# A weight stream whose rounded half is written by a converting DMA of the GpSimd queue

## The chip, the cores and the metric

The kernel runs on one core of a Trainium2 chip, as one program in one launch. The core has a TensorE for matrix products (PE in the profile, with PEld for its weight loads), a VectorE (DVE), a ScalarE (ACT), a GpSimd (POOL), a SyncE (SP) that here only issues transfers, and 16 DMA engines that all queues share. Each of these engines executes its own instructions in order. The metric is the time of one execution on the device in microseconds. Lower is better.

## The reference, cut to what matters

The program is a trunk of two decoder layers over 512 tokens with a model width of 1024, all in float32.

```python
for l in range(DEPTH):                       # DEPTH = 2
    hn = rms_norm(h, attn_norm[l])
    proj = hn @ w_in[l]                      # 1024 x 2592
    y_a = rwkv7_mixer(proj[..., :896], ...)  # 4 heads, a recurrence over the tokens
    y_b = retention_mixer(proj[..., 896:1920], positions)
    y_c = mla_mixer(proj[..., 1920:], ...)   # 8 heads of latent attention
    mix = concatenate([y_a, y_b, y_c], axis=-1)
    h = h + mix @ w_out[l]                   # 1024 x 1024
    hn = rms_norm(h, ffn_norm[l])
    gu = hn @ w_gate_up[l]                   # 1024 x 5632
    h = h + (silu(gu[..., :2816]) * gu[..., 2816:]) @ w_down[l]   # 2816 x 1024
return rms_norm(h, final_norm)
```

## The kernel before, in words

Activations lie transposed, features on the 128 partitions and the 512 tokens along the free dimension. Every large product is made in three passes. An operand is split into a rounded half `hi`, of type float32r, and the rest `lo = x - hi`; the product is then `hi*hi + hi*lo + lo*hi`. In `gemm` (L385) these are three matmuls for each slice of 128 input features, the third of which reads `lo` of the weights. A block of 8 slices is therefore 24 matmuls of 128 x 128 by 512 columns.

The weights were put by the host into the order in which they are used, in one long array, and pass through the chip as a stream of blocks, most of them 128 x 1024 values (512 KB). `load_next` (L361) handles one block. It takes three tiles, each from three buffers: `wr` for the raw float32 values, `wh` for `hi`, `wl` for `lo`. SP loads `wr` from HBM (L373), ACT copies it with a conversion into `wh` (L376), and DVE subtracts to make `wl` (L377). Four blocks, listed in POOL_LO, subtract on POOL. The first two blocks are handled in two parts each.

`wnext` (L380) hands out one block and calls `load_next` so that the next ones are under way: at most three blocks are ready at a time. As `wh` and `wl` have three buffers, the writing of block n+2 waits until TensorE has finished block n-1, and has the time of blocks n and n+1 to be done.

Each layer has two stages. In the mixing stage (some 280 us a layer) the input projection, the three mixers and the output projection are interleaved: the generator `dense` (L899) issues the stream's products, and generators for the recurrence (`rwkv`, `chain` with L741, L746 and L750), retention and attention (`head`, L865 to L870) are woven between them by a driver with a table `T` of waiting times. In the FFN stage, gate and up blocks (L1188 to L1193) alternate, in groups of 8, 8 and 6 feature blocks, and after each group come 8 blocks of the down projection, each added into the residual stream on DVE (L1197). In the FFN POOL multiplies gate and up (L1191), ACT rounds the result (L286) and DVE makes its rest (L287).

The order of TensorE's instructions is that of the program text. On the other engines a planner places each instruction by its own costs once it sees the inputs of that instruction as ready, so their order can differ from that of the text. On the chip each engine then keeps the planner's order and waits where an input is late.

Of the kernel before, what the change touches and what calls it, by code (L numbers as in the profile page):

```python
# [178 lines left out]
def tile_trunk(ctx: ExitStack, tc: tile.TileContext, a: dict, out: bass.AP, dbg=None):  # L179
    nc = tc.nc  # L180
    act, dve, pool, sp = nc.scalar, nc.vector, nc.gpsimd, nc.sync
# [20 lines left out]
    def nm(s):  # L202
        uid[0] += 1
        return f"{s}_{uid[0]}"
# [156 lines left out]
    def load_next(parts=1):  # L361
        if stream["next"] < len(shapes):
            i, j = shapes[stream["next"]]
            stream["next"] += 1
            t = wp.tile([P, i * j], F32, tag="wr", name=nm("wr"), bufs=NW)
            src = a["wts"][stream["off"] : stream["off"] + P * i * j].rearrange("(p n) -> p n", p=P)
            stream["off"] += P * i * j
            hi = wp.tile([P, i * j], F32R, tag="wh", name=nm("wh"))
            lo = wp.tile([P, i * j], F32R, tag="wl", name=nm("wl"))
            on = stream["next"] - 1  # L370
            for part in range(parts):
                z = slice(part * i * j // parts, (part + 1) * i * j // parts)
                stream["dma"] = sp.dma_start(t[:, z], src[:, z])  # L373
                if parts > 1:
                    tc.keep_in_program_order(stream["dma"])
                act.copy(hi[:, z], t[:, z])  # L376
                (pool if on in POOL_LO else dve).tensor_tensor(lo[:, z], t[:, z], hi[:, z].bitcast(F32), ALU.subtract)  # L377
            stream["ready"].append(tuple(z.rearrange("p (i j) -> p i j", i=i) for z in (hi, lo)))

    def wnext():  # L380
        while len(stream["ready"]) < 3 and stream["next"] < len(shapes):
            load_next()
        return stream["ready"].pop(0)
# [515 lines left out]
    def dense():  # L899
# [3 lines left out]
        for k in range(KT):  # L903
            if k < 2:
                tc.keep_in_program_order(sp.dma_start(h[0][:, k, :], a["xT"][:, k, :]))
                load_next(2) if k == 0 else None
            elif k % 2 == 0:
                tc.keep_in_program_order(sp.dma_start(h[k // 2], a["xT"][:, k : k + 2, :]))
                load_next(2) if k == 4 else None
            xg.append(pair(ua))  # L910
            act.activation(xg[k][0], hk(k), AF.Identity, scale=col("attn_norm", 0, k))
            dve.scalar_tensor_tensor(xg[k][1], hk(k), col("attn_norm", 0, k), xg[k][0].bitcast(F32), ALU.mult, ALU.subtract)
# [342 lines left out]
```

## Time and profile before

| | |
|---|---|
| time, median of 3 runs | 1383.34 us (1379.25 to 1384.71) |
| the profiled execution | 1382.67 us, its span 1380.9 us |
| TensorE (PE) busy | 1313.5 us, 95% of the span |
| VectorE (DVE) busy | 796.2 us, 58% |
| ScalarE (ACT) busy | 569.7 us, 41% |
| GpSimd (POOL) busy | 238.7 us, 17% |
| the copies into `wh` (L376, ACT) | 206, 208.2 us busy |
| the subtractions into `wl` (L377, DVE) | 202, 283.3 us busy |
| moved by DMA | 130.84 MB, 95 GB/s over the span |

The profile is that of one execution. Busy time is the time in which an engine executes an instruction; DMA-issuing instructions and waits aren't counted. In a group line the name of a tile stands without its number, so `wh` is any of its buffers, and "a<-b" says that a is written from b. The number after the bar is the busy time of the group, then the mean of one instruction in ns, then the idle time of the engine just before these instructions and which instruction ended it. A timeline row has start (us from the span's start), duration, engine, line and shape, and in brackets the idle time before it. The chain is the sequence of instructions and transfers that ended last, followed back from the end, so its shares say which lines set the time.

### The profile page before, as it was taken

The numbers are of one execution on the slowest core, as the hardware profiler recorded it, in microseconds if no ns is written. First come the engines' busy times: TensorE is split into PE (matmuls) and PEld (weight loads), VectorE is DVE, ScalarE is ACT, GpSimd is POOL, SyncE is SP. The second block draws the span as 40 slices with busy tenths as digits, with TensorE's granted clock in tenths as the row PEclk, the third lists the DMA queues.
The fourth block names the chain that finished last, engine by engine and source line by source line (L and its number), as shares of the span: only waits on it lengthen the run. The fifth ranks groups of instructions, "written<-read, shape, count | busy, mean of one in ns | idle before, by whom it ended". The sixth has DMA issues, their size and how long they took to land.

```text
span 1380.9 us, 16829 instructions
## 1 busy us (share of the span) xinstructions
PE 1313.5 (95%) x6478; PEld 1055.3 (76%) x6478; DVE 796.2 (58%) x1183; ACT 569.7 (41%) x944; POOL 238.7 (17%) x181
## 2 busy tenths in 40 slices
PE   7989988899999999999999898889999999999996
PEld 5778766578888888888877776756888888888884
DVE  7787856747544445344757696476564534543543
ACT  7844445826322232122575335367342212321333
POOL 1160321213110011001314401112131101100111
PEclk9999999999999999999999899999999999999998
DMA  6434421212222232322532424021233223333221
GB/s 235 125 99 140 96 76 32 77 61 92 97 102 92 92 107 92 101 97 73 174 97 81 111 85 85 31 85 54 76 107 105 94 92 95 104 93 105 89 80 61
DMA packets 65577, 130.84 MB, mean 95 GB/s; under 512 B 29044, under 2 KB 31764, under 8 KB 65496
## 3 DMA queue, kind: packets, MB, share of 16 engines
q1 hardware_dynamic: 64120, 128.14, 30.2%
q8 instruction: 51, 0.84, 0.3%
q10 hardware_dynamic: 1232, 1.09, 0.2%
q0 software_dynamic: 144, 0.52, 0.1%
q14 instruction: 30, 0.25, 0.1%
HBM read 117.40 MB, written 9.18 MB: 92 GB/s over the span
## 4 chain that ended last, share of the span: by engine, by line
PE 80%; DVE 10%; ACT 5%; issue 3%; POOL 1%; DMA 1%; SPq 0%; DVEq 0%; ACTq 0%; POOLq 0%
PE pd L232 72%; PE pm L232 7%; PE pm L239 1%; DVE wl L377 1%; DVE nmx L865 1%; DVE Sb L750 1%; ACT u L867 1%; ACT wh L376 1%; DVE u L608 1%; DMA wr<-in_wts_dram 0%; DVE r L296 0%; ACT L327 0%; ACT u L882 0%; DMA u<-in_xT_dram 0%; DVE u L609 0%
## 5 line engine op out<-in xcount | busy, mean ns | idle before, releaser
L232 PE MATMUL pd<-u,wh 128*128 128x512 f32 x3048 | 959.9, 396 | 7.6 <-ACT wh L376 6.4
L232 PEld LDWEIGHTS pd<-u,wh 128*128 128x128 f32 x3048 | 570.0, 189 | 135.3 <-issue 8.0
L232 PE MATMUL pd<-u,wl 128*128 128x512 f32 x1524 | 597.7, 392 | 0.0
L376 ACT CAST wh<-wr 128x1024 fp32r<-128x1024 f32 (+3 forms) x206 | 208.2, 1013 | 531.9 <-PE pd L232 353.9
L232 PEld LDWEIGHTS pd<-u,wl 128*128 128x128 f32 x1524 | 288.5, 189 | 61.0 <-DVE wl L377 0.2
L377 DVE TENSOR_TENSOR wl<-wr,wh 128x1024 fp32r<-128x1024 f32 (+3 forms) x202 | 283.3, 1404 | 59.8 <-ACT wh L376 57.0
L1191 POOL TENSOR_TENSOR r<-r,r 128x512 f32<-128x512 f32 x44 | 63.7, 1447 | 576.2 <-ACT wh L376 484.6
L1190 DVE TENSOR_TENSOR r<-pd,rB 128x512 f32<-128x512 f32 x44 | 30.4, 691 | 135.4 <-PE pd L232 135.4
L1197 DVE TENSOR_TENSOR u<-u,pd 128x512 f32<-128x512 f32 x48 | 33.0, 687 | 125.9 <-PE pd L232 125.9
L232 PE MATMUL pm<-u,u 32*32 32x32 f32 (+4 forms) x728 | 77.2, 287 | 24.9 <-DVE Sb L750 16.2
L232 PEld LDWEIGHTS pm<-u,u 32*32 32x32 f32 (+3 forms) x728 | 55.1, 162 | 48.6 <-DVE Sb L750 21.5
L316 POOL TENSOR_TENSOR acc<-acc,r 128x512 f32<-128x512 f32 x37 | 55.2, 1491 | 192.5 <-ACT r L315 192.1
L1188 DVE TENSOR_TENSOR r<-pd,rB 128x512 f32<-128x512 f32 x44 | 30.4, 691 | 67.7 <-PE pd L232 67.5
L286 ACT CAST u<-r 128x512 fp32r<-128x512 f32 x52 | 32.4, 623 | 78.5 <-POOL r L1191 63.5
L232 PE MATMUL pd<-u,u 96*128 96x512 f32 (+3 forms) x128 | 45.2, 459 | 2.7 <-ACT u L867 1.6
L287 DVE TENSOR_TENSOR u<-r,u 128x512 fp32r<-128x512 f32 x52 | 35.9, 689 | 18.9 <-ACT u L286 18.9
L239 PE MATMUL pm<-ident,u 128*128 128x128 f32 x188 | 33.5, 283 | 5.5 <-ACT r L773 2.0
L870 POOL TENSOR_SCALAR u<-u,rs 128x384 f32<-128x384 f32 x16 | 20.6, 1285 | 98.8 <-DVE rs L869 67.6
L865 DVE TENSOR_REDUCE nmx<-pd 128x1 f32<-128x256 f32 (+3 forms) x64 | 30.0, 481 | 11.7 <-PE pd L232 11.2
L239 PEld LDWEIGHTS pm<-ident,u 128*128 128x128 f32 x188 | 23.7, 145 | 13.1 <-ACT r L773 3.3
L321 DVE SCALAR_TENSOR_TENSOR u<-u,PC,u 128x512 fp32r<-128x512 f32 x24 | 32.0, 1342 | 2.6 <-ACT u L320 2.5
L867 ACT ACTIVATE u<-pd,nmx 128x512 f32<-128x512 f32 (+2 forms) x48 | 26.0, 546 | 11.9 <-DVE nmx L865 7.8
(243 smaller groups left out, 1142.9 us busy)
## 6 DMA issues: line engine op xcount, KB each, us to landing
wr<-in_wts_dram SPq DMA_DIRECT2D x174, 512.0 KB, 3.5
wr<-in_wts_dram SPq DMA_DIRECT2D x22, 384.0 KB, 3.1
u<-in_xT_dram SPq DMA_DIRECT2D x7, 512.0 KB, 6.7
tb<-tab_d SPq DMA_DIRECT2D x8, 256.0 KB, 4.9
r<-r SPq DMA_DIRECT2D x32, 64.0 KB, 2.0
h_d<-u SPq DMA_DIRECT2D x4, 512.0 KB, 2.6
u<-h_d SPq DMA_DIRECT2D x4, 512.0 KB, 3.6
wr<-in_wts_dram SPq DMA_DIRECT2D x4, 432.0 KB, 3.1
```

Of the source, the lines that this page charges most:

```text
L232: tc.keep_in_program_order(nc.tensor.matmul(o, lhsT, rhs, start=start, stop=stop, skip_group_check=True))
L239: tc.keep_in_program_order(nc.tensor.transpose(o, x, idn))
L286: act.copy(hi, src)
L287: E("e273").tensor_tensor(lo, src, hi.bitcast(F32), ALU.subtract)
L316: E("e302").tensor_tensor(acc, acc, q, ALU.add)
L321: dve.scalar_tensor_tensor(lo, t, g, hi.bitcast(F32), ALU.mult, ALU.subtract)
L376: act.copy(hi[:, z], t[:, z])
L377: (pool if on in POOL_LO else dve).tensor_tensor(lo[:, z], t[:, z], hi[:, z].bitcast(F32), ALU.subtract)
L865: dve.tensor_reduce(nmx, ps[:, 0:w], AX.X, ALU.max, negate=True)
L867: act.activation(pp[ib], ps[:, 0:w], AF.Exp, bias=nmx, accum_out=ssum)
L1191: E("e1171").tensor_tensor(t, t, u, ALU.mult)
L1197: dve.tensor_tensor(hk(m), hk(m), ps, ALU.add)
```

## The change

One statement of `load_next` changes. Where ACT copied the landed tile `wr` into `wh`, a DMA issued from POOL's queue reads the same weights from HBM and writes them to `wh`, converting from float32 to float32r on the way. The load into `wr` stays, as the subtraction still reads it. So each weight block is read from HBM twice, once on SP's queue and once on POOL's.

```diff
                 stream["dma"] = sp.dma_start(t[:, z], src[:, z])
                 if parts > 1:
                     tc.keep_in_program_order(stream["dma"])
-                act.copy(hi[:, z], t[:, z])
+                pool.dma_start(hi[:, z], src[:, z])
                 (pool if on in POOL_LO else dve).tensor_tensor(lo[:, z], t[:, z], hi[:, z].bitcast(F32), ALU.subtract)
```

## The prediction

> **What bounds the kernel now.** I read the stages first: busy time by stretch (PE, PEld, DVE, ACT, POOL, granted clock, DMA share, GB/s), for the first layer's mixing stage, its FFN and the second layer's mixing stage, and then what the chain of waits holds in the whole run and in each.
>
> ```profile
> 35.00:315.00 280.00, 256.60 (x1504) 201.31 (x1503) 196.84 (x386) 148.81 (x298) 62.04 (x48) 0.96 0.31 87
> 315.00:700.00 385.00, 384.64 (x1691) 316.96 (x1690) 190.53 (x186) 124.09 (x154) 56.54 (x37) 1.00 0.31 101
> 700.00:985.00 285.00, 261.89 (x1513) 202.47 (x1513) 196.43 (x384) 148.44 (x299) 61.14 (x49) 0.97 0.28 80
> by line: PE pd L232 71.7%; PE pm L232 7.0%; issue 2.6%; PE pm L239 1.2%; DVE wl L377 1.0%; DVE nmx L865 1.0%; DVE Sb L750 0.6%; ACT u L867 0.6%; ACT wh L376 0.6%; DVE u L608 0.5%; DMA wr<-in_wts_dram 0.5%; DVE r L296 0.4%; ACT L327 0.4%; AC
> by line: PE pd L232 46.4%; PE pm L232 16.6%; issue 3.9%; PE pm L239 3.8%; DVE wl L377 1.8%; DVE nmx L865 1.6%; DVE Sb L750 1.5%; ACT u L867 1.2%; DVE u L608 1.1%; POOL r L776 1.0%; DVE r L330 1.0%; DVE r L329 0.9%; DVE r L296 0.9%; DVE u L6
> by line: PE pd L232 98.5%; POOL r L1191 0.5%; PE pm L232 0.4%; DVE u L287 0.2%; DVE r L1190 0.2%; ACT u L286 0.2%; issue 0.1%; POOLq L1191 0.0%; POOLq L316 0.0%
> by line: PE pd L232 37.0%; PE pm L232 16.2%; issue 6.9%; DVE nmx L865 3.1%; DVE wl L377 2.3%; PE pm L239 2.0%; ACT wh L376 1.7%; ACT u L867 1.7%; DVE u L608 1.5%; ACT L327 1.4%; DVE Sb L750 1.3%; DVE r L296 1.2%; ACT u L882 1.1%; DVE u L609
> ```
>
> The FFN is TensorE's alone: 384.6 of 385 us busy, and products are 98.5% of the chain. No copy can be gained there, only lost. The mixing stages are latency chains with DVE at 70%; in them L377 is on the chain with 1.8% of 280 = 5.0 us and 2.3% of 285 = 6.6 us. The copy that goes, L376, is 0.6% of the whole chain, 8.3 us, although ACT spends 208 us on it:
>
> ```profile
> L376 ACT CAST wh<-wr 128x1024 fp32r<-128x1024 f32 (+3 forms) x206 | 208.2, 1013 | 531.9 <-PE pd L232 353.9
> L377 DVE TENSOR_TENSOR wl<-wr,wh 128x1024 fp32r<-128x1024 f32 (+3 forms) x202 | 283.3, 1404 | 59.8 <-ACT wh L376 57.0
> 413.75 0.61 PE L232 MATMUL pd<-u,wh 128*128 128x512 f32 x2
> 413.77 1.05 ACT L376 CAST wh<-wr 128x1024 fp32r<-128x1024 f32 x1 [3.86 <-issue]
> 413.95 0.69 DVE L1190 TENSOR_TENSOR r<-pd,rB 128x512 f32<-128x512 f32 x1 [3.31 <-PE pd L232]
> 414.81 1.29 POOL L1191 TENSOR_TENSOR r<-r,r 128x512 f32<-128x512 f32 x1 [9.59 <-ACT wh L376]
> 414.86 2.33 DVE L377 TENSOR_TENSOR wl<-wr,wh 128x1024 fp32r<-128x1024 f32 x1 [0.21 <-ACT wh L376]
> 416.14 0.62 ACT L286 CAST u<-r 128x512 fp32r<-128x512 f32 x1 [1.31 <-POOL r L1191]
> 417.11 0.68 DVE L287 TENSOR_TENSOR u<-r,u 128x512 fp32r<-128x512 f32 x1
> 419.21 1.05 ACT L376 CAST wh<-wr 128x1024 fp32r<-128x1024 f32 x1 [2.45 <-PE pd L232]
> ```
>
> These are the last gate-and-up block of an FFN group and the first down block. TensorE starts block n at 413.75, and with that the buffer of block n-1 is free: the copy for block n+2 starts at once and the subtraction follows 1.09 us after it. Blocks come every 419.21 - 413.77 = 5.44 us, so block n+2 is needed 10.88 us after the copy may start. Weights are ready some 7 us early.
>
> **The price of the new transfer.** The trace has one DMA of POOL, 512 KB (to HBM, without conversion), and plain loads of 512 KB on SP, quiet and crowded.
>
> ```profile
> L561 POOL DMA_DIRECT2D vf_d<-u x1: 749/749/749, 48.2 to 48.2; - x1
> DMA to landing us min/median/max: 4.0/4.0/4.0
> wr<-in_wts_dram SPq DMA_DIRECT2D x174, 512.0 KB, 3.5
> u<-in_xT_dram SPq DMA_DIRECT2D x7, 512.0 KB, 6.7
> q1 hardware_dynamic: 64120, 128.14, 30.2%
> ```
>
> A converting load isn't shown. Lower bound 3.5 us, upper 6.7; I take 4.1, POOL's own row and 0.1 for the semaphore, as it has the same queue and size. Then `wh` is there 4.1 us after the release instead of 1.09: 3.0 us later. POOL pays 206 x 0.75 = 154 us of issuing beside 239 us of work, in a span of 1381: it has the room.
>
> The Trainium skill, page "DMA: Bandwidth & Descriptors", section "Anatomy of one DMA — SWDGE (gpsimd) path", fits about 2.0 us plus bytes over 436 GB/s, an estimate of 3.2 us here, under the row's 4.0. By it the wait would be 2.2 us instead of 3.0, the third term below 10.3 instead of 14.1, and the sum 3.8 us lower.
>
> **The change part by part.**
>
> Start. The DMA engines are already full while the first blocks and x come in.
>
> ```profile
> 5.00:10.00 5.00, 3.54 (x7) 1.84 (x7) 3.06 (x6) 3.52 (x7) 0.00 (x0) 1.00 1.00 310
> 10.00:15.00 5.00, 5.00 (x12) 3.46 (x13) 4.70 (x7) 4.51 (x8) 0.00 (x0) 1.00 1.03 404
> 2.12 4.46 DMA u<-in_xT_dram
> 6.60 6.26 DMA wr<-in_wts_dram
> 12.88 1.05 ACT wh L376
> ```
>
> The chain is a transfer until 12.88. Three `wh` buffers are free from the beginning, so three more blocks, 1.5 MB, join: 1.5 MB at 404 GB/s = +3.7 us. Ends: 0 if DVE's work behind it takes up the delay, 4.8 at 310 GB/s.
>
> FFN, steady. Release + 4.1 + 1.23 (the subtraction's 2.33 falls to 1.23 when L1191 isn't beside it) = 5.3 us against 10.88: nothing, at the upper bound too (6.7 + 2.33 = 9.0). What hides it is two blocks of products. Without that cover it would be 3 us on each of some 140 blocks. SP's next load waits for the subtraction that frees `wr`, 3 us later; a load is issued three blocks ahead, so that costs nothing.
>
> FFN, group ends. Behind the waiting subtraction on DVE stands L287, the rest of the last activation. Its reader is the second matmul of the down block's eighth slice, the 23rd of 24: 413.75 + 22 x 5.44/24 = 418.74. It was ready at 417.79. If the order stays: 413.77 + 4.1 + 1.23 + 0.68 = 419.78, 1.0 us late. In the groups of six TensorE waits for it already:
>
> ```profile
> 653.31 0.69 DVE L1190 TENSOR_TENSOR r<-pd,rB 128x512 f32<-128x512 f32 x1 [3.79 <-PE pd L232]
> 654.00 0.96 DVE L377 TENSOR_TENSOR wl<-wr,wh 128x768 fp32r<-128x768 f32 x1
> 656.78 0.69 DVE L287 TENSOR_TENSOR u<-r,u 128x512 fp32r<-128x512 f32 x1 [1.83 <-ACT u L286]
> 653.13 0.84 ACT L376 CAST wh<-wr 128x768 fp32r<-128x768 f32 x1 [3.90 <-PE pd L232]
> ```
>
> There 653.13 + 4.1 + 0.96 + 0.69 = 658.9 against 657.5, 1.4 us late. Four ends of 1.0 and two of 1.4 make 7.0 us. The planner may put L287 first, so I take half: +3.5 (ends 0 and 7).
>
> Mixing. This is the main term. DVE stands still at each subtraction until the transfer lands, with the recurrence (L741, L750), the softmax (L865) and evictions behind it, and TensorE waits for those.
>
> ```profile
> 188.56 0.83 ACT L376 CAST wh<-wr 128x768 fp32r<-128x768 f32 x1 [0.54 <-PE pd L232]
> 189.43 0.96 DVE L377 TENSOR_TENSOR wl<-wr,wh 128x768 fp32r<-128x768 f32 x1 [1.67 <-ACT wh L376]
> 190.31 0.35 DVE L750 SCALAR_TENSOR_TENSOR Sb<-pm,dsc,EX 128x128 f32<-128x128 f32 x1
> 35.00:315.00 280.00, 33.42 (x27) 4.90 (x2) 0.96 0.31 87
> 700.00:985.00 285.00, 35.66 (x29) 0.45 (x1) 0.97 0.28 80
> ACT wh L376 <- PE pd L232: 30.8, 12, 8.5
> ACT wh L376 <- PE pd L232: 37.5, 16, 4.8
> ```
>
> ```profile
> 7.58 0.16 DVE L427 CAST posk<-poski 128x4 f32<-128x4 int32 x1
> ```
>
> (Rows 4 and 5: DVE and POOL busy in L377 by stage; 6 and 7: how long, how often and at most how long ACT waited for the release, first mixing stage and second.) In 12 + 16 = 28 blocks the copy stood waiting for the release, so there the transfer's delay shows in full: 28 x 3.0 = 84 us of DVE waiting. What part reaches the end? Of L377's busy time 5.0 of 33.4 and 6.6 of 35.7 us are on the chain, 15% and 18%, mean 0.168: 84 x 0.168 = +14.1 us. Ends: 0 if the planner puts ready work first (it does reorder: L427, written far behind the loop of L912, runs at 7.58 between two of its rounds), and 28 x 5.6 x 0.168 = 26.3 at 6.7 us.
>
> POOL now waits for those releases, 68 us in all, with L870, L316 and the retention's products behind it; its largest line on the chain is 1.0%, so that is under 1 us, taken as nothing.
>
> Gone from ACT: 8.3 us of the chain, -8.3 (ends 0 and -16.6, if what ACT does next moves up as far).
>
> Sum against the profiled execution: 1382.67 + 3.7 + 3.5 + 14.1 - 8.3 = 1395.7 us. The runs' median is 0.7 above it, inside their spread; no correction.
>
> The same page, section "Queues, rings and completion order", says that a DMA engine takes turns between queues packet by packet, so POOL's load and SP's next one would share where they overlap. The 6.7 us of x beside other loads agrees; by that the mixing term would go toward 26.3 and the time toward 1408.
>
> **The rivals.**
>
> Hidden. The planner knows a transfer as late and puts L377 behind other ready DVE work; the 14.1 go: 1381.6. For it: the reordering above. Against: L377 has until now stood right behind the copy.
>
> Faster. ACT's in-order queue is the one place: the copy leaves it, its 8.3 us leave the chain, and neither start nor group ends pay as DVE's own work covers both: 1374.4. For it: 1.7% of the second mixing stage. It decides where `wh` lands before DVE reaches its subtraction, at about 1.1 us after the release in the 28 blocks, or with the planner's help. Against: no row lands in under 3.5.
>
> Transfers bind. SP's 128 MB take 30.2% of the engines; at that price the second reading (at most 206 x 0.524 = 108 MB) adds 25%. A conversion of more than 2.3 times the price fills an FFN block (0.31 x 5.44 = 1.7 us plus 2.3 x 1.7 = 5.6); at three times it is 6.7 us, 1.3 us more on some 140 blocks: 1382.67 + 182 = 1565. Nothing shows a converting transfer, so neither for nor against.
>
> That the transfer copies without rounding would leave every count and wait as it is, and the time too.
>
> **How the numbers follow.** Forecast 52%, own range 1386 to 1412; hidden 17%; faster 18%; transfers bind 13%. A measurement here tells about 0.5%, 6.9 us, from no change: 1376.4 to 1390.3. Of the forecast 44 points lie above that and 8 inside; the hidden case is inside; of the faster one 16 points are below: slower 57%, same 27%, faster 16%. The range 1371 to 1445 takes in all but the best end of the faster case and most of the binding one.
>
> **What would show it.** Right: L377 in both mixing stages with idle time before it ended by the transfer, of the order of 84 us; L377's share of the chain up, L376 gone; DMA share in the FFN near 0.6 with TensorE still full; the first products some 4 us later. Wrong: L377 without waits for `wh`; an FFN block longer than 5.44 us; landings of `wh` far from 4 us; POOL's lines on the chain.

## The result and the profile after

The changed kernel takes 1419.71 us, the kernel before, run beside it, 1381.3 us: a ratio of 1.0265 (95% interval 1.0216 to 1.0314). It is slower, as forecast, but by three times as much. The profile below is that of a second series of the same kernel (1422.05 us, ratio 1.0281, 1.0257 to 1.0305, the first experiment below), because the profiled execution of the first series ran at a mean granted clock of 0.653 and took 1901.78 us. Its execution took 1421.38 us, 38.7 us more than the one before; the spans differ by the same 38.7.

From the page of the changed kernel: span, busy times, the two lines of the weight stream, the DMA issues (size, median us to landing) and the queues (packets, MB, share of 16 engines).

```profile
span 1419.6 us, 16924 instructions
PE 1325.6 (93%) x6478; PEld 1060.6 (75%) x6478; DVE 750.6 (53%) x1183; ACT 370.8 (26%) x738; POOL 339.1 (24%) x387
q1 hardware_dynamic: 64120, 128.14, 28.4%
q0 software_dynamic: 29808, 103.82, 23.5%
L377 DVE TENSOR_TENSOR wl<-wr,wh 128x1024 fp32r<-128x1024 f32 (+3 forms) x202 | 249.7, 1237 | 386.1 <-DMA wh<-in_wts_dram 194.7
L376 POOL DMA_DIRECT2D wh<-in_wts_dram x206 | 114.4, 556 | 744.4 <-PE pd L232 688.8
wh<-in_wts_dram POOLq DMA_DIRECT2D x174, 512.0 KB, 4.4
u<-in_xT_dram SPq DMA_DIRECT2D x7, 512.0 KB, 8.4
```

The copies left ACT (569.7 us busy before, 370.8 now), and 194.7 us of DVE's idle time are now ended by the landing of `wh`; before, 57.0 us were ended by ACT's copy. POOL's 339.1 us hold the 114.4 us in which it issues the transfers: POOL's issuing is counted as busy here, against what stands ahead of the profile before, and its other work fell from 238.7 to 224.7 us. One thing in the first lines matters more than it seems to. TensorE does the same 6478 matmuls but is busy for 1325.6 us instead of 1313.5: 12.1 of the 38.7 us are matmuls that ran longer. The other 26.6 are idle time (span less busy: 67.4 before, 94.0 now).

The same stages as in the prediction, cut where the stages now lie (columns as there):

```profile
35.00:332.00 297.00, 266.73 (x1546) 208.86 (x1545) 203.52 (x395) 129.55 (x279) 77.07 (x79) 0.96 0.45 133
332.00:718.00 386.00, 384.78 (x1689) 316.22 (x1688) 165.81 (x185) 50.20 (x79) 87.30 (x108) 1.00 0.60 197
718.00:1023.00 305.00, 271.33 (x1514) 208.10 (x1513) 195.19 (x383) 122.79 (x271) 77.19 (x77) 0.94 0.41 120
```

The FFN is unhurt: TensorE is full for 384.78 of 386 us beside a DMA share that doubled to 0.60. In the second mixing stage the same work (1513 and 1514 matmuls) takes 305 us instead of 285; of these 20 us, 9.4 are longer busy time (271.33 against 261.89) at a granted clock of 0.94 instead of 0.97, and 10.6 are idle.

How late TensorE is can be followed through the program, as its order is that of the text in both kernels. Worked out from the starts of the same matmul, counted from 0, in both traces:

```
matmul no.   where                        before     after    late by
  100        start                          35.2      44.9       9.7
 1800        first FFN under way           360.7     378.3      17.5
 3100        end of the first FFN          655.4     672.9      17.6
 5100        second FFN under way         1053.0    1092.1      39.0
 end                                      1380.9    1419.6      38.7
```

So the start costs 9.7 us, the first mixing stage 7.8, the second 21.4, and the two FFN stages nothing.

The waits of DVE and POOL in the two mixing stages (total us, times, longest), the first two rows of the first stage, the others of the second:

```profile
DVE wl L377 <- DMA wh<-in_wts_dram: 17.7, 13, 3.7
POOL wh L376 <- PE pd L232: 95.3, 20, 8.9
DVE wl L377 <- DMA wh<-in_wts_dram: 42.7, 17, 8.6
POOL wh L376 <- PE pd L232: 100.1, 16, 13.5
```

Before, in the same two stages, DVE stood there for ACT's copy:

```profile
DVE wl L377 <- ACT wh L376: 4.7, 6, 2.4
DVE wl L377 <- ACT wh L376: 20.4, 7, 8.2
```

So DVE stands for 60.4 us in 30 waits for a landing, where it stood for 25.1 us in 13 waits for the copy: 35.3 us were added. Counted by all idle time of DVE just before the subtraction, whatever ended it, it is 73.5 us against 27.7, so 45.8 more. The mixing stages lose 29.2 us. In the chain of waits the transfer is now the largest entry that isn't TensorE's or "issue":

```profile
by line: PE pd L232 30.9%; issue 13.7%; PE pm L232 11.1%; DMA wh<-in_wts_dram 8.0%; PE pm L239 3.3%; DVE wl L377 2.2%; ACT u L867 1.5%; DMA r<-r 1.5%; DVE Sb L750 1.2%; POOL u L612 1.2%; DMA xs_d<-r 1.1%; DVE r L329 1.1%; POOL r L776 1.0%; 
```

That is 8.0% of 297 = 23.8 us in the first mixing stage. It isn't a price: the chain counts a transfer from its issue to its landing, while DVE only stood for 17.7 us there, and the stage lost 7.8.

**The start.** Timeline rows of the changed kernel, TensorE and POOL:

```profile
14.46 1.58 PE L232 MATMUL pd<-u,wh 128*128 128x512 f32 x2 [1.90 <-ACT u L911]
26.73 0.59 POOL L376 DMA_DIRECT2D wh<-in_wts_dram  x1 [4.50 <-PE pd L232]
27.33 1.31 POOL L316 TENSOR_TENSOR acc<-acc,r 128x512 f32<-128x512 f32 x1
29.16 2.68 POOL L316 TENSOR_TENSOR acc<-acc,r 128x512 f32<-128x512 f32 x2
31.90 1.24 PE L232 MATMUL pm<-acc,C 128*128 128x512 f32 x2 [3.21 <-POOL acc L316]
```

The first and the last of these matmuls before:

```profile
9.74 1.58 PE L232 MATMUL pd<-u,wh 128*128 128x512 f32 x2
23.96 1.02 PE L232 MATMUL pm<-acc,C 128*128 128x512 f32 x2
```

Two delays follow each other. The first row's matmul begins 4.7 us later than before: the `wh` transfers of the first blocks share the engines with x, which now lands in 8.4 us instead of 6.7. Then the sum of squares of the normalization, `acc` on POOL (L316), stands in POOL's queue behind the transfer of block 3, which waits 4.50 us for the release of its buffer. TensorE, which reads `acc`, waits 3.21 us, and its matmul begins 7.9 us later than before.

**The clock.** The longest of the new slow stretches, in the second mixing stage: DVE and TensorE rows of the timeline, then busy times and clock (the column before the last two) in five stretches.

```profile
943.19 1.23 DVE L377 TENSOR_TENSOR wl<-wr,wh 128x1024 fp32r<-128x1024 f32 x1 [0.32 <-DMA wh<-in_wts_dram]
944.34 1.48 DVE L865 TENSOR_REDUCE nmx<-pd 128x1 f32<-128x512 f32 x3
945.85 0.69 DVE L1130 TENSOR_TENSOR u<-pd,fB 64x512 f32<-64x512 f32 x1
946.69 0.46 PE L232 MATMUL pd<-u,u 96*128 96x128 f32 x2 [2.31 <-DVE u L1130]
```

```profile
943.00:947.40 4.40, 2.09 (x12) 1.28 (x11) 3.48 (x6) 2.02 (x7) 0.00 (x0) 1.00 0.41 128
947.40:950.80 3.40, 3.40 (x8) 1.51 (x7) 2.80 (x10) 1.24 (x4) 1.24 (x1) 0.52 0.12 30
950.80:954.20 3.40, 3.40 (x9) 1.83 (x8) 1.84 (x8) 1.70 (x6) 1.24 (x1) 0.50 0.00 0
954.20:957.60 3.40, 3.40 (x11) 2.27 (x10) 2.63 (x11) 2.02 (x6) 0.25 (x1) 0.50 0.00 0
957.60:961.00 3.40, 2.69 (x11) 1.76 (x10) 1.55 (x6) 2.54 (x6) 1.58 (x2) 0.97 0.01 2
```

DVE waits only 0.32 us for the landing here, and makes `wl` ahead of the softmax and rotation work (L865, L1130) that TensorE needs. TensorE stands for 2.31 us, and then runs at half its clock for 10.2 us, though busy throughout: some 5.1 us lost behind one idle gap. Summed over slices of 1 us, each by its length times one less its clock, the clock costs 8.5 us in the second mixing stage before and 18.7 after, in the first 10.2 in both, and 1.7 at the start after the gap at 31.90. The Trainium skill, page "TensorE: Matmul & The Clock Gate", section "What's actually happening", says that the array falls to half its clock after an idle window of about 3.4 us and comes back after a busy one. The trace agrees on the half (0.50) and on steps of 3.4 us (its stretches at half clock in the mixing stages last 3.4, 6.8 or 10.2 us); it differs in that a gap of 2.31 us was enough here, and that three windows passed before the clock came back. In steps of 3.41 us counted from the drop at 947.55, the gap lies within one step, in which TensorE is busy for 1.10 us. In the kernel before, a gap of 2.59 us (from 856.22) falls across two such steps, counted from that trace's own drops, busy for 1.92 and 1.57 us, and the clock stays at 1.00. That suggests that the share within a step counts and not the length of the gap; but in the same trace the clock also drops at 717.77, after a step in which TensorE is busy throughout, so it isn't shown.

### The profile page after: what moved, and what is told of

Read it like the earlier page. It is cut to its first block, busy times and chain, and to the rows that moved or that the text cites. A ratio compares the mean times of both kernels' runs of the same rounds, so it can differ in the third digit from the quotient of the medians.

```text
span 1900.0 us, 16924 instructions
## 1 busy us (share of the span) xinstructions
PE 1844.4 (97%) x6478; PEld 1195.6 (63%) x6478; DVE 762.0 (40%) x1183; ACT 372.6 (20%) x738; POOL 338.1 (18%) x387
## 3 DMA queue, kind: packets, MB, share of 16 engines
q1 hardware_dynamic: 64120, 128.14, 22.0%
q0 software_dynamic: 29808, 103.82, 18.7%
q10 hardware_dynamic: 1232, 1.09, 0.2%
## 4 chain that ended last, share of the span: by engine, by line
PE 91%; DVE 3%; DMA 2%; issue 2%; POOL 1%; ACT 1%; SPq 0%; DVEq 0%; POOLq 0%; ACTq 0%
PE pd L232 80%; PE pm L232 9%; PE pm L239 2%; DMA wh<-in_wts_dram 1%; DVE Sb L750 0%; DMA u<-in_xT_dram 0%; DMA poski<-in_posT_dram 0%; POOL u L612 0%; DMA r<-in_positions_dram 0%; DVE wl L377 0%; DVE r L1226 0%; DVE nmx L865 0%; DVE u L1081 0%; POOL acc L316 0%; POOL r L776 0%
## 5 line engine op out<-in xcount | busy, mean ns | idle before, releaser
L232 PE MATMUL pd<-u,wh 128*128 128x512 f32 x3048 | 1285.8, 512 | 9.6 <-DMA wh<-in_wts_dram 6.5
L232 PEld LDWEIGHTS pd<-u,wh 128*128 128x128 f32 x3048 | 632.5, 210 | 366.4 <-issue 126.3
L232 PE MATMUL pd<-u,wl 128*128 128x512 f32 x1524 | 773.4, 507 | 0.0
L232 PEld LDWEIGHTS pd<-u,wl 128*128 128x128 f32 x1524 | 316.8, 208 | 177.1 <-issue 58.2
L377 DVE TENSOR_TENSOR wl<-wr,wh 128x1024 fp32r<-128x1024 f32 (+3 forms) x202 | 244.3, 1210 | 375.9 <-DMA wh<-in_wts_dram 359.3
L376 POOL DMA_DIRECT2D wh<-in_wts_dram x206 | 114.4, 556 | 1259.8 <-PE pd L232 1200.5
L1189 ACT ACTIVATE r<-r 128x512 f32<-128x512 f32 x44 | 27.8, 632 | 487.5 <-DVE r L1188 487.5
L232 PE MATMUL pm<-u,u 32*32 32x32 f32 (+4 forms) x728 | 95.9, 335 | 18.0 <-DVE Sb L750 13.9
L232 PEld LDWEIGHTS pm<-u,u 32*32 32x32 f32 (+3 forms) x728 | 64.3, 186 | 57.1 <-issue 23.2
L287 DVE TENSOR_TENSOR u<-r,u 128x512 fp32r<-128x512 f32 x52 | 36.3, 699 | 91.5 <-ACT u L286 91.3
L232 PE MATMUL pd<-u,u 96*128 96x512 f32 (+3 forms) x128 | 62.9, 613 | 1.3 <-DVE u L1130 1.3
L316 POOL TENSOR_TENSOR acc<-acc,r 128x512 f32<-128x512 f32 x37 | 52.5, 1420 | 47.7 <-ACT r L315 45.4
L239 PE MATMUL pm<-ident,u 128*128 128x128 f32 x188 | 43.1, 345 | 2.4 <-DVE u L870 0.7
L865 DVE TENSOR_REDUCE nmx<-pd 128x1 f32<-128x256 f32 (+3 forms) x64 | 30.8, 486 | 26.1 <-PE pd L232 25.8
```

The lines of the kernel that those rows point to most:

```text
L232: tc.keep_in_program_order(nc.tensor.matmul(o, lhsT, rhs, start=start, stop=stop, skip_group_check=True))
L239: tc.keep_in_program_order(nc.tensor.transpose(o, x, idn))
L287: E("e273").tensor_tensor(lo, src, hi.bitcast(F32), ALU.subtract)
L316: E("e302").tensor_tensor(acc, acc, q, ALU.add)
L376: pool.dma_start(hi[:, z], src[:, z])
L865: dve.tensor_reduce(nmx, ps[:, 0:w], AX.X, ALU.max, negate=True)
```

## The experiments

The expectations set several theories against each other. D, called W in the first ones: the loss is DVE standing at the landing in the mixing stages, with everything queued behind it. T: the second reading costs wherever weights stream. Q: it is POOL's queue, whose own work stands behind transfers that wait for a release. O: it is only that the planner, with other instructions to place, orders them otherwise. Beside them stands the start of the program, where D or Q may act. The ratio is to the kernel before, run beside each kernel, with its 95% interval. No kernel here leaves out work.

O has something to act on. Compared instruction by instruction, by tile and shape, 66 of DVE's 981 instructions other than the subtractions stand at another place in the sequence than before; where a kernel's order bears on its result, the same count is given below.

**Where the loss lies: each stage alone.**

The changed kernel again:

> The changed kernel itself once more, timed, and for a profile at the usual clock. Theory W (in the mixing stages DVE stands at each subtraction until the converted block lands): 1410 to 1425, with the added time inside the two mixing stages and the FFN at 5.44 us a block. Theory T (twice the reading costs time wherever weights stream, through the DMA engines or the granted clock): the same total, but the added time spread over all blocks, about 140 of 206 parts of it in the FFN.

1422.05 us, ratio 1.0281 (1.0257 to 1.0305).

Transfers only in the FFN blocks:

```diff
-                pool.dma_start(hi[:, z], src[:, z])
+                if on % 102 >= 34:
+                    pool.dma_start(hi[:, z], src[:, z])
+                else:
+                    act.copy(hi[:, z], t[:, z])
```

> The converting transfer only for the FFN's 136 blocks, the ScalarE copy for the 68 of the mixing stages and the start. W: 1381 to 1388, at most the 7 us of the group ends over before. T: about two thirds of the loss, 1405.

1382.4 us, ratio 0.9993 (0.9977 to 1.001). In the 136 FFN transfers the change is free, and it gains nothing either, though ACT is busy 135 us less (434.6 instead of 569.7). T falls.

Transfers only in the others (`on % 102 < 34`):

> The converting transfer only for the 68 blocks of the mixing stages (with the start), the ScalarE copy in the FFN. W: nearly all of the loss, 1408 to 1420. T: a third of it, 1393.

1420.8 us, ratio 1.027 (1.0253 to 1.0288): the whole loss comes from 70 of 206 transfers, those of the start and the mixing stages.

The first three blocks by the ACT copy (`if on >= 3:` around the transfer):

> As the changed kernel, but the first three blocks by the ScalarE copy, so that no POOL transfer competes with x at the start. If the start costs what was predicted, 3 to 5 us under the changed kernel; if DVE's work behind it covers the delay, no difference.

1422.34 us, ratio 1.0285 (1.0268 to 1.0303): nothing gained. The first three transfers alone aren't the start's loss: TensorE is still 6.9 us late at matmul 100, as the `acc` sums still stand behind the transfer of block 3.

**POOL's queue alone.** The kernel before, where in the start and mixing blocks POOL waits for the release of `wl` with a tiny write, which stands in its queue as the transfer would (a part of Q and not of D or O):

```diff
+                if on % 102 < 34:
+                    pool.memset(lo[:, z][:, 0:2].bitcast(F32), 0.0)
                 act.copy(hi[:, z], t[:, z])
```

> The kernel before, and in the mixing stages' blocks POOL first clears two columns of wl, so its queue stands at the release of the buffer as in the changed kernel, but no transfer follows; ScalarE still copies. Theory D (the loss is DVE waiting for the landing of wh): 1380 to 1387. Theory Q (the loss is POOL's queue standing at the release, with its adds and products behind): 1400 to 1420. Theory O (it is only that the planner orders the instructions otherwise): cannot say, within 1375 to 1400.

1385.17 us, ratio 1.0013 (0.9995 to 1.0031). TensorE is 4.7 us late at matmul 100 and 2.1 at 5100. POOL stands at the release for 215.5 us in the two mixing stages (195.4 in the changed kernel), and DVE's order is that of the kernel before throughout, so this is a clean test of the queue. The start shows it at work,

```profile
28.57 1.13 PE L232 MATMUL pm<-acc,C 128*128 128x512 f32 x2 [2.95 <-POOL acc L316]
```

the mixing stages show no loss. Q falls as the main cause.

**The landing without POOL.** The kernel before, with ACT's copy kept, but the subtraction of the start and mixing blocks reads the raw weights from a second, plain load issued on ACT's queue behind the copy (the tile needs room, so `wr` has two buffers instead of three):

```diff
-                act.copy(hi[:, z], t[:, z])
-                (pool if on in POOL_LO else dve).tensor_tensor(lo[:, z], t[:, z], hi[:, z].bitcast(F32), ALU.subtract)
+                if on % 102 < 34:
+                    cp = act.copy(hi[:, z], t[:, z])
+                    raw = wp.tile([P, i * j], F32, tag="wx", name=nm("wx"), bufs=1)[:, z]
+                    with tc.issue_after(cp.ins):
+                        act.dma_start(raw, src[:, z])
...
+                (pool if on in POOL_LO else dve).tensor_tensor(lo[:, z], raw, hi[:, z].bitcast(F32), ALU.subtract)
```

> The kernel before, and in the mixing stages' blocks the subtraction reads its raw weights from a second plain load, issued from ScalarE's queue right behind the copy, so DVE waits some 4 us longer than before for each and the bytes double, while POOL's queue has none of it; the raw tile has two buffers instead of three to make room. D: 1405 to 1425. Q: 1380 to 1390. O: cannot say.

1445.11 us, ratio 1.045 (1.0418 to 1.0481). Waits in the first and second mixing stage:

```profile
DVE wl L384 <- DMA wx<-in_wts_dram: 17.8, 10, 5.2
DVE wl L384 <- DMA wx<-in_wts_dram: 28.4, 12, 8.4
```

So a load that lands late costs as much without a conversion and without POOL's queue. It isn't a pure test of D, and it lies 20 us above D's range: DVE waits less here than in the changed kernel (46.2 us against 60.4) and the loss is larger. In the trace ACT's queue stands for at least 24 us, at 20 of its 70 issues, until the single buffer is free, with its own work behind it, and how much of the 62 us is that isn't known. The control, the kernel before with `NW = 2` alone:

> The control to d1_act_dma: the kernel before with two buffers for wr instead of three. If two raw buffers alone cost what c4_wh4_act lost: 1392 to 1405, and d1_act_dma's second load some 45 us on top. If the fourth wh buffer was to blame there: 1378 to 1388.

1383.8 us, ratio 1.0012 (0.9999 to 1.0025): the smaller `wr` isn't the cause.

**Taking the wait from DVE: a fourth buffer.** With four `wh` buffers the transfer may start a block earlier. The changed kernel, with `wr` cut to two for room:

```diff
-NU, NR, NW = 29, 8, 3
+NU, NR, NW = 29, 8, 2
-            hi = wp.tile([P, i * j], F32R, tag="wh", name=nm("wh"))
+            hi = wp.tile([P, i * j], F32R, tag="wh", name=nm("wh"), bufs=4)
```

> The changed kernel with four buffers for wh and two for wr: each converting transfer may start a block (5.4 us) earlier, so it should land before DVE comes to the subtraction, and POOL stands at an older release. D and Q: 1380 to 1395, the loss mostly gone. O: 1410 to 1425, as the order is still not that of before.

1404.4 us, ratio 1.015 (1.0121 to 1.0179): 17.7 us of the 39 come back, less than D and more than O expected. The waits for a landing are all but gone, with none in the first mixing stage, and in the second (700 to 1040 us)

```profile
DVE wl L377 <- DMA wh<-in_wts_dram: 14.0, 3, 9.7
```

From matmul 100 to 5100 TensorE loses 11.3 us instead of 29.3 (22.5 less 11.2, and 39.0 less 9.7). This is the best evidence for D: with the waits, 18 us of the mixing stages' loss went. It doesn't shut out O, as DVE's order is neither that of the changed kernel nor that of before (70 of the 981 stand elsewhere in either comparison). The same edit on the kernel before:

> The control to the last one: the kernel before with four buffers for wh and two for wr. All theories: within 0.5% of before, 1376 to 1390.

1398.12 us, ratio 1.0101 (1.0067 to 1.0135), outside what was expected. Its rows (first and second mixing stage) show that the edit has a price of its own:

```profile
ACT wh L376 <- DMA wr<-in_wts_dram: 18.6, 8, 4.9
ACT wh L376 <- DMA wr<-in_wts_dram: 20.5, 7, 5.3
```

With four `wh` and two `wr` buffers ACT reaches its copy before the load has landed, and stands there with its other work behind it; two `wr` buffers alone cost nothing. So the comparison of these two kernels, 6 us, doesn't measure the landing.

**Moving the wait to another engine.** The changed kernel, where POOL also makes `wl` of the mixing blocks:

```diff
-                (pool if on in POOL_LO else dve).tensor_tensor(lo[:, z], t[:, z], hi[:, z].bitcast(F32), ALU.subtract)
+                (pool if on in POOL_LO or 5 <= on % 102 < 34 else dve).tensor_tensor(lo[:, z], t[:, z], hi[:, z].bitcast(F32), ALU.subtract)
```

> The changed kernel, with the subtractions of the mixing stages' blocks (but for the first five) on POOL instead of DVE: the same transfers with the same landings, but POOL waits for them and not DVE. Theory D (DVE's wait for the landing): 1380 to 1395. Theory O (the loss comes from the order the planner gives, or from the bytes): 1410 or more. If POOL's own work is then held up by the waits, something between.

1447.71 us, ratio 1.0482 (1.0456 to 1.0508): D's expectation missed by over 50 us. DVE hardly waits for a landing in the mixing stages (8.2 us), but POOL does, needs 2297 ns for what takes DVE 1237, and has critical work behind it:

```profile
PE pm L232 <- POOL u L612: 12.6, 4, 7.7
PE pd L232 <- POOL wl L377: 7.0, 7, 2.0
```

So D is too narrow where it names DVE. How much of this is POOL's wait and how much its slower subtraction isn't separated here.

**Placing the subtraction later.** The changed kernel, where each subtraction is written into the program one block later, when its transfer has had a block's time (the first three as before):

```diff
-                (pool if on in POOL_LO else dve).tensor_tensor(lo[:, z], t[:, z], hi[:, z].bitcast(F32), ALU.subtract)
+                def sub(z=z, t=t, hi=hi, lo=lo, on=on):
+                    (pool if on in POOL_LO else dve).tensor_tensor(lo[:, z], t[:, z], hi[:, z].bitcast(F32), ALU.subtract)
...
     def wnext():
+        while stream["late"]:
+            stream["late"].pop(0)()
```

> The changed kernel, with the subtraction of a block written one block later in the program, so that on DVE it has more work ahead of it and finds its block landed. D: 1383 to 1398, of which up to 10 are the start. O: 1410 or more.

1410.04 us, ratio 1.0204 (1.0181 to 1.0227): 12 us better than the changed kernel, but not the 1383 to 1398 of D; O had said 1410 or more. The waits and the busy time say why both are so (first and second mixing stage, then the page's busy line):

```profile
DVE wl L379 <- DMA wh<-in_wts_dram: 25.2, 11, 6.3
DVE wl L379 <- DMA wh<-in_wts_dram: 38.3, 18, 8.5
```

```profile
span 1407.8 us, 16926 instructions
PE 1317.2 (94%) x6478; PEld 1057.2 (75%) x6478; DVE 753.8 (54%) x1183; ACT 370.7 (26%) x738; POOL 339.1 (24%) x387
```

DVE waits as long as in the changed kernel, 63.5 us in 29 waits: the planner hardly moved the subtraction, and 1174 of DVE's 1183 instructions follow each other as there. What fell is the busy time of TensorE, by 8.4 us against the changed kernel, and its idle time by 3.4 (94.0 to 90.6). The gain is mostly clock. So nine instructions at other places, with the same waits, are worth 12 us, nearly all of it in the second mixing stage: from matmul 100 to 5100 TensorE loses 17.8 us here and 29.3 there. The length of the waits alone doesn't set the price. The same edit on the kernel before changes next to nothing, the order (1179 of 1183 instructions as before) or the time:

> The control: the kernel before (ScalarE copy) with the same later subtraction. D: within 1% of before, 1370 to 1395, and not far under f1_late_sub.

1381.92 us, ratio 0.9999 (0.9985 to 1.0013).

**The start, properly taken out.** The same with the first six blocks by the ACT copy, so that no transfer stands ahead of the `acc` sums:

> f1_late_sub with the first six blocks by the ScalarE copy, so that no transfer of POOL runs beside x and the first adds of POOL stand behind no release. By D with the start as seen in the profile of the changed kernel (TensorE's hundredth product 9.7 us late): 5 to 10 us under f1_late_sub; if the later stages take it back, no difference.

1400.99 us, ratio 1.0154 (1.0119 to 1.0189). 1410.04 - 1400.99 = 9.0 us, by the two intervals some 6 us either way: the start's 9.7 us are, as far as this tells, still there at the end. The matmul that began at 31.90 is back near its old place:

```profile
24.17 1.02 PE L232 MATMUL pm<-acc,C 128*128 128x512 f32 x2
```

**Both remedies.** Four `wh` buffers, two `wr`, the first six blocks by ACT:

> The changed kernel with four buffers for wh and two for wr, and the first six blocks by the ScalarE copy. If DVE's wait for the landing and the start are the whole loss, this stands level with c4_wh4_act (the same buffers, ScalarE copy in all): 1388 to 1402. If something else of the change costs, above 1402.

1396.49 us, ratio 1.0109 (1.0072 to 1.0145): 7.9 us under four buffers alone, and level with the kernel before in the same buffers (1398.12), as expected if the waits and the start were the whole loss; but that kernel has ACT's waits in their place, so the level is weak evidence. And with three `wr` again (one tile of another pool given up for the room, `NU = 28`):

> As w5_wh4_start with the third buffer of wr back, paid for with one of the 29 large activation buffers. If the waits are the whole loss and that buffer isn't missed: 1372 to 1388, level with the kernel before or under it. If the buffer is missed: 1390 to 1420.

1404.86 us, ratio 1.0153 (1.0118 to 1.0188). The expectation had 1372 to 1388 if the waits were the whole loss, and 1390 to 1420 if the tile that was given up is missed. So either something else costs, or the third `wr` buffer's gain and that tile's price offset each other; no run has `NU = 28` alone. The profiled execution of this kernel took 1397.47 us and was the fastest of four, the others 1404.61 to 1406.95; DVE's waits in it are down to 4.3 us in the first mixing stage and 24.0 in the second:

```profile
DVE wl L380 <- DMA wh<-in_wts_dram: 4.3, 1, 4.3
DVE wl L380 <- DMA wh<-in_wts_dram: 24.0, 3, 9.3
796.52 1.14 POOL L377 DMA_DIRECT2D wh<-in_wts_dram  x2 [6.77 <-PE pm L232]
802.98 1.23 DVE L380 TENSOR_TENSOR wl<-wr,wh 128x1024 fp32r<-128x1024 f32 x1 [7.95 <-DMA wh<-in_wts_dram]
```

In the last two rows the release comes late, after a stretch in which TensorE did other work, and two transfers are issued at once at 796.52: the subtraction then waits 7.95 us. One buffer more didn't hide this landing.

The profiled executions side by side; idle and busy are TensorE's, against the kernel before, and clock is its mean over the execution:

| kernel | time, ratio | late at no. 100 / 1800 / 5100 | idle | busy | clock |
|---|---|---|---|---|---|
| changed | 1.0281 | 9.7 / 17.5 / 39.0 | +26.6 | +12.1 | 0.974 |
| first three blocks by ACT | 1.0285 | 6.9 / 14.5 / 38.2 | +24.2 | +13.5 | 0.972 |
| plain load on ACT's queue | 1.045 | 9.9 / 29.0 / 60.7 | +37.9 | +22.4 | 0.967 |
| subtraction on POOL | 1.0482 | 10.1 / 29.4 / 69.9 | +43.0 | +26.3 | 0.965 |
| later subtraction | 1.0204 | 9.4 / 16.6 / 27.2 | +23.2 | +3.7 | 0.979 |
| and six blocks by ACT | 1.0154 | 0.2 / 6.9 / 18.9 | +15.3 | +3.0 | 0.980 |
| four `wh` | 1.015 | 11.2 / 15.7 / 22.5 | +18.3 | +4.2 | 0.979 |
| and six blocks by ACT | 1.0109 | 1.5 / 9.1 / 14.9 | +14.4 | +0.5 | 0.980 |
| four `wh`, three `wr`, six by ACT | 1.0153 (this execution 1.0113) | 0.7 / 3.6 / 14.9 | +13.7 | +1.1 | 0.981 |
| transfers in the FFN only | 0.9993 | 2.0 / 2.6 / 2.9 | +4.1 | -1.6 | 0.985 |
| kernel before | 1 | 0 | 67.4 | 1313.5 | 0.982 |

Busy time times mean clock is 1288 to 1293 us in every one of them (1313.5 x 0.982 = 1290; 1325.6 x 0.974 = 1291; 1339.8 x 0.965 = 1293). As the same matmuls give the same product to within 5 us, the large differences in TensorE's busy time are its clock; those of under some 4 us are inside that spread. None of these kernels is faster than the one before.

## Why the prediction was right or wrong

The direction was right and the size was not: +13.0 us in the sum, 38.7 in the trace, of which 9.7 at the start, 29.2 in the mixing stages with the copy's relief in it, and nothing in the FFN. The forecast's own range, 1386 to 1412, misses the result. By steps:

- **FFN, steady: nothing.** Right, and for the reason given (384.78 of 386 us busy; FFN transfers alone 0.9993).
- **Group ends: 3.5.** Nothing: between matmuls 1800 and 3100, with group ends among them, TensorE loses 0.1 us. The planner did what the prediction left open, and put L287 ahead of the next subtraction:

```profile
434.72 0.62 ACT L286 CAST u<-r 128x512 fp32r<-128x512 f32 x1 [7.09 <-POOL r L1191]
435.37 0.69 DVE L287 TENSOR_TENSOR u<-r,u 128x512 fp32r<-128x512 f32 x1 [2.15 <-ACT u L286]
435.98 1.22 DVE L377 TENSOR_TENSOR wl<-wr,wh 128x1024 fp32r<-128x1024 f32 x1
```

- **The landing, 4.1 us.** Right: 4.4, against the bounds of 3.5 and 6.7. The issue took 556 ns, not 749, so POOL issues for 114 us instead of 154. The estimate by the Trainium skill, page "DMA: Bandwidth & Descriptors", section "Anatomy of one DMA — SWDGE (gpsimd) path", is 3.2 us for 512 KB; the trace has 4.4, beside a second stream of the same size.
- **The start, 3.7 us.** 9.7 at matmul 100, and worth some 9.0 at the end. The engines' share was near (4.7 at matmul no. 6; the bounds went to 4.8). What is missing is the step "POOL now waits for those releases ... taken as nothing". It looked at POOL's share of the chain, not at what would stand behind the first waiting transfer: L316, which TensorE needs at once. In the mixing stages the same step holds (the wait alone on POOL: 1.0013, of which the start is a part).
- **Mixing, 84 x 0.168 = 14.1.** This is the step that failed, in both factors and in opposite ways. The 84 us were to be added standing. The waits for a landing are 60.4 us in 30 waits, near in number to the 28, but DVE had stood for 25.1 us in these stages before: 35.3 us were added, or 45.8 by all idle time just before the subtraction, about half of the 84. The share was not 0.168: the 29.2 us that were lost are 0.64 to 0.83 of what was added, with whatever ACT's relief gave already inside. That the two errors partly cancel is luck, and still the 29.2 lie beyond the term's own upper end of 26.3, which held the size of a wait open but not the share. A share of busy time on the old chain says where the old subtraction set the end, and not what a standing DVE holds up; behind it stood the recurrence, the softmax and the evictions, as the prediction itself had listed. And no term of the sum had TensorE's clock: of the 12.1 us of longer busy time 9.4 lie in the second mixing stage, almost half of its loss. The mixing stages lost some 19 us to idle time (26.6 less about 8 at the start) and some 10 to the clock.
- **ACT's copy, -8.3.** Not seen. In the FFN the relief of 135 us gave nothing; in the mixing stages it can't be told apart from the rest. In part it was counted twice: of the seven pieces of L376 on the old chain, 7.7 us in all, four with 4.0 us are followed by L377, and the 3.0 us of the mixing term are already net of the copy's 1.09.
- **The rivals.** Hidden, 1381.6: no, DVE waits 60.4 us. Faster, 1374.4: no run was. Transfers bind, 1565: no; the converting queue took 23.5% of the engines for 103.82 MB, 0.226% for each MB, the plain one 28.4% for 128.14 MB, 0.222%.

What is shown: the loss comes from the transfers of the start and the mixing stages, and POOL's queue alone doesn't make it. What stays open is how much of the mixing stages' 29.2 us is DVE's standing (D) and how much the planner's other order (O). No run keeps DVE's order and changes its waits. For D: with the waits nearly gone, 18 of the 29 us went, and 36 of the 981 instructions moved (two `wr` buffers alone) cost nothing. For O: at the same waits nine moved instructions were worth 12 us. Open too is why the second mixing stage pays 21.4 us and the first 7.8; the added waits don't give it (22.3 and 13.0 us for a landing, 19.7 and 26.1 by all idle time before the subtraction). That the gaps bring the half clock is read from their sequence in the traces; no run held TensorE busy through a gap.

## What to carry to other kernels

What a wait on an engine that executes in order costs depends on what stands behind it in the queue. So list that work at each place, take off the waits that were there before, and don't scale by the engine's old share of the chain. The same holds for the queue of the engine that issues a transfer; here it cost at the start. In this kernel's FFN, with two blocks of matmuls to cover a transfer, the transfer was free; in its mixing stages, chains of short steps, replacing an on-chip copy of 1 us by a transfer of 4.4 us cost 29 us, although the copying engine was relieved. And if the scheduler can reorder, compare the orders of the two kernels before putting a difference down to a wait. Split a change of TensorE's time into idle and busy first: if the same matmuls are busy for longer, the gaps have cost clock as well.

## What the hardware showed that was not expected

- A gap of 2.31 us in TensorE's work was followed by 10.2 us at half the clock. In the slower kernels the clock is 0.5 to 26.3 us of the loss, and the larger part of what the later subtraction gave back (8.4 of 11.8 us by busy time, 7.0 by the granted clock).
- The conversion from float32 to float32r costs the DMA engines little: 0.226% of their time for each MB against 0.222% on SP's queue, whose packets are of other sizes too. For packets of 4096 bytes alone the trace has 204.5 ns against 193.5, 6% more.
- POOL issues the converting transfer in 556 ns, against 749 for its earlier store.
- The subtraction on DVE falls from 1404 to 1237 ns in the mean. A block of 128x1024 takes 1.22 us in both kernels while POOL doesn't compute; beside POOL's work it took 1.99 us in the mean before, and that is the case for 60 of the 170 blocks before and for 15 after.
